# An adaLN block with RG-LRU, forgetting attention and SwiGLU: the upper feed-forward products with tokens standing and 512 weight columns moving

## The chip, the cores and the metric

The kernel runs on one core of a Trainium2 chip. The metric is the device time in microseconds (us); the median of three runs of the kernel before is 2051.7. Engines are called PE (TensorE), DVE (VectorE), ACT (ScalarE), POOL (GpSimd) and SP (SyncE, which here issues DMA transfers); PEld is TensorE's weight load, which overlaps its matmuls.

## The reference

One transformer-like block on 512 tokens of width 2048, in float32. Around it lie six modulation vectors from the condition `c`; the sixth, gt2, gates the last residual add:

```python
mod = c_act @ w_ada[l] + b_ada[l]
sh1, sc1, gt1, sh2, sc2, gt2 = jnp.split(mod, 6, axis=-1)
h = modulate(rms_norm(x, g_mix[l]), sh1, sc1)
proj = h @ w_in[l]
...
x = x + gt1[:, None, :] * (mix @ w_out[l])
h2 = modulate(rms_norm(x, g_ffn[l]), sh2, sc2)
gate, up = jnp.split(h2 @ w_up[l], 2, axis=-1)
x = x + gt2[:, None, :] * ((jax.nn.silu(gate) * up) @ w_down[l])
```

Between `proj` and `mix` stand a gated linear recurrence and an attention with forget gates. `w_up` is 2048 x 11264 (gate and up halves of 5632 = 44 x 128 features), `w_down` 5632 x 2048.

## The kernel before

Every large product is made of float32 data split in two: a high part (an ACT copy that rounds, L234) and a low part (a DVE subtraction, L235), and three matmuls: high by high, high by low, low by high. Raw weights come by DMA into buffers of 128x2048 (two in the pool `raw`, two in `raw2`); halves of 1024 are split into rings of three pages each for the high and the low parts (`wsplit`). So a split waits until TensorE is done with the third split before it.

The program runs through these stages: the input projection, the attention heads, the recurrence, the output projection wo0 to wo3 (from 540.6 us to 724.4), two groups of feed-forward features by ordinary products (up0, up1), the other 40 features of 128 each by fast products ("upper", 816 to 1622 us), and the down projection in four phases (1622 to 2044 us). During the early stages DVE also works off a queue of modulation blocks: `ada_block` loads 128x2048 of `w_ada` in two halves and multiplies and sums them against the broadcast `c_b` (L159, L169); tables such as `WO_ADA` say at which steps a block is taken from the queue.

The upper products use the seven products of a fast 2x2 scheme: gate and up features by token halves of 256, input dimension in halves. For each feature block f the weights (four blocks of 128x512 per chunk, two chunks) are summed on DVE (L1108, L1109, L1112), split, and then used as the standing operand: 128x128 of weights stand, 256 tokens move, 168 matmuls a feature (L1131). The token combinations, called T[p] and in the rows ta to tg, were split earlier. Four PSUM banks hold the seven products of a feature, and its results are formed by DVE (L1146 to L1150, L1152) and ACT (L1151), with features on the partitions, as the down projection wants them. `keep_act` then folds pairs of results for the down phases and sends them to DRAM (`td`).

In the same loop 64 pieces of gt2 (128x512, L189) are taken one after each chunk, loaded through ACT's DMA queue, and the sums of down weights that two products want (`s2d`, `s4d`) are made by accumulating DMA.

The down phases also use seven products: 4 and 5, then 1 and 7, then 6, then 2 and 3, each over q = 0 to 10. In a step q of the first two phases the first product's weights lie in `raw`, the second's in `raw2`; the second's are the sum of both, made in place on DVE (L1187). In phase 0 the order on all engines is product 4 of q, product 5 of q, product 4 of q + 1. Each product of a step is 24 matmuls of 512 columns with tokens standing (`dn_mm`, through L239).

The order of each engine's instructions comes from the order of the code, moved by priorities (`AHEAD` = 2000 puts loads and splits ahead, `EVAC` = 2500 the copies that free PSUM) and by `issue_after`, which ties an instruction behind another.

## Time and profile before

| what | value |
|---|---|
| runs of the kernel before | 2051.39, 2051.70, 2052.81 us (median 2051.7) |
| the profiled execution | 2049.87 us |
| its span in the trace | 2048.2 us |
| PE / DVE / ACT busy | 2030.6 / 1707.4 / 944.7 us |
| granted TensorE clock | 0.998 |
| upper products, 816 to 1622 us | PE 806.00 busy, DVE 711.65, ACT 341.32 |
| down phase 0, 1622 to 1742 us | PE 118.67 busy, DVE 91.96 |
| down phase 1, 1742 to 1862 us | PE 120.00 busy, DVE 90.38 |

The busy time of an engine counts its instructions' own time, waits left out. The chain of work that ended last is followed back from the last instruction, at each step to what released it; the share of an engine in it says how much of the span it set. In a timeline a row gives the start and length of an instruction, its line in the code, its output and inputs (without buffer numbers), and in brackets how long its engine had been idle and what ended that. For a DMA, landing is counted from its issue.

### The profile page before, as it was taken

To read this page: it belongs to the slowest core of one execution; us is meant where nothing else is said; L and a number is where in the kernel's file an instruction comes from. 1 tells how busy PE (TensorE), PEld (TensorE's weight loads), DVE (VectorE), ACT (ScalarE), POOL (GpSimd) and SP (SyncE) were. 2 spreads that over 40 slices of the span, in tenths; PEclk is the share of its full clock that TensorE was granted. 3 is DMA by queue.
4 is the path that set the end of the run, shared out by engine and by line. 5 is a ranking of instruction groups with operands and counts; after the bars stand their busy time and mean duration, and the time that the engine had idled before them with its cause. 6 is when DMAs were issued, how large, how long until landed. Compare 5 with 4: busy or idle time off the path is not lost.

```text
span 2048.2 us, 32491 instructions
## 1 busy us (share of the span) xinstructions
PE 2030.6 (99%) x12529; PEld 1850.5 (90%) x12529; DVE 1707.4 (83%) x2560; ACT 944.7 (46%) x1321; POOL 98.1 (5%) x126
## 2 busy tenths in 40 slices
PE   9999999999999999999999999999999999999999
PEld 7889998888888888999999999999999978888887
DVE  8999769887687669888898888989888877777796
ACT  4433447765522266444444444444444355545443
POOL 0000000111000000001000000000000000000000
PEclk9999999999999999999999999999999999999999
DMA  9989766767588852448988888988888587777894
GB/s 351 356 299 328 247 224 225 228 210 260 181 294 302 286 175 101 134 134 235 264 230 239 238 232 246 251 244 232 245 235 227 165 281 236 238 252 240 280 326 167
DMA packets 175822, 493.36 MB, mean 241 GB/s; under 512 B 20625, under 2 KB 45105, under 8 KB 171570
## 3 DMA queue, kind: packets, MB, share of 16 engines
q1 hardware_dynamic: 156162, 437.68, 63.1%
q0 software_dynamic: 10144, 36.70, 9.6%
q10 hardware_dynamic: 9360, 16.89, 2.4%
q8 instruction: 98, 1.61, 0.3%
q14 instruction: 58, 0.48, 0.1%
...
## 4 chain that ended last, share of the span: by engine, by line
PE 90%; DVE 4%; issue 2%; DMA 2%; SPq 0%; ACT 0%; POOL 0%; DVEq 0%; ACTq 0%; POOLq 0%
PE w1p L239 4%; PE dn6p L239 3%; PE dn3p L239 3%; PE dn2p L239 3%; PE dn7p L239 3%; PE dn1p L239 3%; PE dn5p L239 3%; PE dn4p L239 2%; PE yr1p L239 2%; PE up0p L239 2%; PE yr0p L239 2%; PE wo2p L239 2%; PE wo3p L239 2%; PE wo1p L239 2%; PE up1p L239 2%
## 5 line engine op out<-in xcount | busy, mean ns | idle before, releaser
L159 DVE SCALAR_TENSOR_TENSOR ada<-ada,c_b 128x1024 f32<-128x1024 f32 x96 | 116.1, 1220 | 26.6 <-DMA ada<-in_adaT 26.5
L234 ACT ACTIVATE uq_0sh<-uq_0r 128x1024 fp32r<-128x1024 f32 x40 | 42.4, 1060 | 116.9 <-DVE uq_0r L1109 113.8
L235 DVE TENSOR_TENSOR uq_0tl<-uq_0r,uq_0th 128x1024 fp32r<-128x1024 f32 x40 | 49.0, 1224 | 37.3 <-ACT uq_0th L234 37.3
L234 ACT ACTIVATE uq_0ah<-uq_0r 128x1024 fp32r<-128x1024 f32 x40 | 42.4, 1060 | 69.2 <-PE uf37p L1131 2.1
L234 ACT ACTIVATE uq_1ah<-uq_1r 128x1024 fp32r<-128x1024 f32 x40 | 42.5, 1062 | 60.6 <-issue 26.3
L235 DVE TENSOR_TENSOR uq_0al<-uq_0r,uq_0ah 128x1024 fp32r<-128x1024 f32 x40 | 49.0, 1224 | 25.5 <-ACT uq_0ah L234 24.2
L1048 POOL DMA_DIRECT2D s2d<-in_wdn x44 | 36.4, 826 | 668.1 <-DMA s2d<-in_wdn 641.1
L235 DVE TENSOR_TENSOR uq_0sl<-uq_0r,uq_0sh 128x1024 fp32r<-128x1024 f32 x40 | 49.0, 1226 | 18.8 <-ACT uq_0sh L234 18.3
L234 ACT ACTIVATE uq_0th<-uq_0r 128x1024 fp32r<-128x1024 f32 x40 | 42.4, 1060 | 45.1 <-DVE uq_0sl L235 2.5
L1151 ACT ACTIVATE ug<-ug 128x512 f32<-128x512 f32 x40 | 25.3, 632 | 81.2 <-DVE ug L1148 81.2
L234 ACT ACTIVATE uq_1th<-uq_1r 128x1024 fp32r<-128x1024 f32 x40 | 42.4, 1061 | 33.8 <-PE uf43p L1131 1.1
L234 ACT ACTIVATE uq_1sh<-uq_1r 128x1024 fp32r<-128x1024 f32 x40 | 42.5, 1062 | 25.3 <-DVE uq_1r L1109 23.8
L235 DVE TENSOR_TENSOR uq_1tl<-uq_1r,uq_1th 128x1024 fp32r<-128x1024 f32 x40 | 48.9, 1222 | 4.9 <-ACT uq_1th L234 3.8
L239 PE MATMUL w1p<-hpl,w1h 128*128 128x512 f32 x128 | 49.8, 389 | 0.0
L239 PE MATMUL w1p<-hph,w1l 128*128 128x512 f32 x128 | 49.8, 389 | 0.0
L235 DVE TENSOR_TENSOR uq_1sl<-uq_1r,uq_1sh 128x1024 fp32r<-128x1024 f32 x40 | 49.0, 1224 | 0.1
L1108 DVE TENSOR_TENSOR uq_0r<-uq_0r 128x1024 f32<-128x1024 f32 x40 | 48.7, 1218 | 0.0
L235 DVE TENSOR_TENSOR uq_1al<-uq_1r,uq_1ah 128x1024 fp32r<-128x1024 f32 x40 | 48.7, 1217 | 0.0
L1108 DVE TENSOR_TENSOR uq_1r<-uq_1r 128x1024 f32<-128x1024 f32 x40 | 48.7, 1217 | 0.0
L189 DVE SCALAR_TENSOR_TENSOR gt<-gt,c_b 128x512 f32<-128x512 f32 x64 | 43.8, 684 | 0.0
L169 DVE SCALAR_TENSOR_TENSOR ada<-ada,c_b 128x1024 f32<-128x1024 f32 x32 | 39.0, 1218 | 5.0 <-DMA ada<-in_adaT 4.9
L239 PE MATMUL w1p<-hph,w1h 128*128 128x512 f32 x128 | 42.4, 391 | 0.0
...
## 6 DMA issues: line engine op xcount, KB each, us to landing
ada<-in_adaT SPq DMA_DIRECT2D x128, 512.0 KB, 5.1
...
gt<-in_adaT ACTq DMA_DIRECT2D x64, 256.0 KB, 5.9
...
```

Of the source, the lines that this page charges most:

```text
L159: nc.vector.scalar_tensor_tensor(out=t, in0=t, scalar=1.0, in1=cs, op0=ALU.mult, op1=ALU.mult, accum_out=ac)
L169: nc.vector.scalar_tensor_tensor(out=t, in0=t, scalar=1.0, in1=c_b[:, cs], op0=ALU.mult, op1=ALU.mult, accum_out=ada_acc[j][:, hf, i:i + 1])
L189: nc.vector.scalar_tensor_tensor(out=t, in0=t, scalar=1.0, in1=c_b[:, r * S:(r + 1) * S], op0=ALU.mult, op1=ALU.mult, accum_out=gt2_acc[:, ...
L234: tail_hi.append(nc.scalar.activation(R(hi[:, :n]), raw_ap, AF.Copy).ins)
L235: tail_lo.append(nc.vector.tensor_sub(R(lo[:, :n]), raw_ap, hi[:, :n]).ins)
L239: nc.tensor.matmul(ps, lhsT=R(l), rhs=R(r), start=start, stop=stop)
L1048: nc.gpsimd.dma_start(out=out[:, cs], in_=src[:, cs], accum_op=ALU.add)
L1108: nc.vector.tensor_add(blocks[:, 0:3:2], blocks[:, 0:2], blocks[:, 2:3].broadcast_to([P, 2, 512]))
L1151: nc.scalar.activation(g, g, AF.Silu)
```

## The change

**Upper products.** The loop over 40 features becomes one over 10 blocks of four features (512 columns). In a block the seven products come one after another, in the order 4, 5, 1, 7, 6, 2, 3. The token combinations are now the standing operand (128x128 of the two halves t), and 512 weight columns move: 48 matmuls a product through the helper `mm` (L245 of the new code), two PSUM banks each. The weights come as four units A, C, B, D of 128x4096 (in two tiles); they are relaid in DRAM for this. Between the products they are summed in place on DVE, 2048 wide (L1130): A += C for product 5, C += B for 7, A += B for 6, D += A for 3. They are split in quarters of 1024. Results now have tokens on the partitions: ACT copies products 4, 5, 1 and 7 out (L1197), DVE folds (L1204, L1206 to L1209, L1214), and the result of Silu (L1217) by the other half (L1218) is turned back by four TensorE transposes a feature into the one bank `rg` (`back`, L1159) and copied by ACT (L1162). The transposes of a block stand in products 5 and 1 of the next; those of the last block in down phase 0.

**Buffers.** `raw2` has four buffers instead of two. `c_b` and some sums move to a pool that ends before the upper products; `c_b` is kept in DRAM and loaded again, in one of `raw2`'s buffers, in down phase 0.

**gt2.** Its first six k-tiles join the queue of modulation blocks (12 operations of 128x1024; `WO_ADA` and the hooks of the stage before wo0 take more blocks at other steps). The other ten make 40 pieces of 128x512 (L194), two a step, from step 2 of down phase 0 to the end of phase 1.

**Down phases.** Phase 0 is skewed: product 4 of q + 1 comes ahead of product 5 of q. The loading of a step (`dn_open`) is parted from its splits (`dn_prod`). The accumulating DMA of `s2d` and `s4d` is spread at other steps of the upper loop (`SUMS_AT`, `SUMS_PER`).

```diff
-WO_ADA = ((11, 14), (0, 4, 8, 12), (0, 3, 6, 9, 12), (0, 3, 6, 9))
+WO_ADA = ((9, 12, 15), (0, 3, 6, 9, 12), (0, 3, 6, 9, 12, 15), (0, 2, 4, 6, 8))
-GT2_AT, SUMS_AT = 16, 14
+GT2_ADA = 6
+SUMS_AT, SUMS_PER = 24, 10
...
+    for i in range(GT2_ADA):
+        pending.append(((GT2, i), lambda i=i: ada_block(GT2, i)))
...
-    bp = ctx.enter_context(tc.tile_pool(name="bp", bufs=2))
+    bp = ctx.enter_context(tc.tile_pool(name="bp", bufs=4))
...
+    ORDER = (4, 5, 1, 7, 6, 2, 3)
...
+    def sum_unit(dst, src):
+        for d_, s_ in zip(dst, src):
+            nc.vector.tensor_add(d_, d_, s_)
...
+            elif p == 5:
+                sum_unit(un[U_A], un[U_C])
...
+        for q in range(4):
+            with tc.high_priority(offset=AHEAD):
+                hi, lo = wsplit(src[q // 2][:, (q % 2) * 1024:(q % 2 + 1) * 1024], 1024, f"up{b}_{p}_{q}")
...
+    def back(g, b, f, last=False):
+        pt = misc(f"up_t{b}_{f}") if last and f else rgp(f"up_t{b}_{f}")
+        for t in range(NT):
+            nc.tensor.transpose(out=pt[:, t * P:(t + 1) * P], in_=g[t][:, f * P:(f + 1) * P], identity=ident)
+        o = page(f"uo{b}_{f}", "d")
+        with tc.high_priority(offset=EVAC):
+            nc.scalar.activation(o, pt, AF.Copy)
+        keep_act(o, 2 * STD + 4 * b + f)
...
-                for k in range(4):
-                    th, tl = T[p][c * 4 + k]
-                    ks = slice(k * P, (k + 1) * P)
-                    for n, (w, x) in enumerate(((hi, th), (hi, tl), (lo, th))):
-                        first, last = c + k + n == 0, c == 1 and k == 3 and n == 2
-                        nc.tensor.matmul(m[p], lhsT=R(w[:, ks]), rhs=R(x), start=first and p in opens, stop=last,
-                                         skip_group_check=True)
+            for j, hi, lo in prod_weights(p, b, un):
+                th, tl = T[p][j]
+                for t in range(2):
+                    c_ = slice(t * P, (t + 1) * P)
+                    mm(ps[t], th[:, c_], hi, j == 0, False)
+                    mm(ps[t], th[:, c_], lo, False, False)
+                    mm(ps[t], tl[:, c_], hi, False, j == 7)
+                for fn in hk.get((i, j), ()):
+                    fn()
...
+        hk = {(1, 1 + 2 * f): [lambda g=s1 + u2, b=b, f=f: back(g, b, f)] for f in range(4)}
...
+        steps = [(q, n) for q in range(NQ) for n in range(len(prods))]
+        if ph == 0:
+            steps.sort(key=lambda x: (x[0] + x[1], x[1]))
...
+                for m in range(2 * (NQ * ph + q - GT2_AT), 2 * (NQ * ph + q - GT2_AT) + 2):
+                    if 0 <= m < 4 * (KT - GT2_ADA):
+                        gt2_piece(m)
```

How the instructions stand now is shown at three places. First TensorE in the upper products. Before, in feature 12 (`uq_0a` and `uq_0c` are weight parts, the trailing h and l mean high and low; `tb` and `tc` are token combinations):

```order
L1131 MATMUL uf12p_9575<-tb2h,uq_0ah 128x256
L1131 MATMUL uf12p_9575<-tb2l,uq_0ah 128x256
L1131 MATMUL uf12p_9575<-tb2h,uq_0al 128x256
L1131 MATMUL uf12p_9575<-tb2h,uq_0ah 128x256
L1131 MATMUL uf12p_9575<-tb2l,uq_0ah 128x256
L1131 MATMUL uf12p_9575<-tb2h,uq_0al 128x256
L1131 MATMUL uf12p_9573<-tc0h,uq_0ch 128x256
```

Now, from the end of product 4 to the start of product 5 of a block (`up_5_0h` are weights, `td0h` tokens, `us_1` results of the block before):

```order
L245 MATMUL up_4p_9465<-up_4_3l,te7h 128x512
L245 MATMUL up_4p_9465<-up_4_3h,te7l 128x512
L245 MATMUL up_5p_9546<-up_5_0h,td0h 128x512
L245 MATMUL up_5p_9547<-up_5_0h,td0h 128x512
L1159 MATMUL up_t_0_9566<-ident,us_10_9146 128x128
L245 MATMUL up_5p_9546<-up_5_0l,td0h 128x512
L245 MATMUL up_5p_9546<-up_5_0h,td0l 128x512
L245 MATMUL up_5p_9547<-up_5_0l,td0h 128x512
```

The operand behind the arrow that moves has 512 columns instead of 256, a product runs to its end before the next begins, and product 5 opens with two matmuls of the high part and a transpose, ahead of the first that wants the low part.

Second DVE in the upper products. Before, between features 12 and 14 (`uq` weights, `ug` and `uu` results, `gt2_3` a piece of gt2):

```order
L235 TENSOR_TENSOR uq13_1sl_9944<-uq13_1r_9930,uq13_1sh_9943 128x1024
L1152 TENSOR_TENSOR ug12_9805<-ug12_9805,uu12_9806 128x512
L235 TENSOR_TENSOR uq13_1tl_9949<-uq13_1r_9930,uq13_1th_9948 128x1024
L189 SCALAR_TENSOR_TENSOR gt2_3_9689,gt2_acc_130<-gt2_3_9689,c_b_81 128x512
L235 TENSOR_TENSOR uq14_0al_10070<-uq14_0r_10066,uq14_0ah_10069 128x1024
L1106 TENSOR_TENSOR uq14_1cl_10187<-uq14_1r_10179,uq14_1ch_10186 128x512
L1108 TENSOR_TENSOR uq14_0r_10066<-uq14_0r_10066 128x2x512
L1109 TENSOR_TENSOR uq14_0r_10066<-uq14_0r_10066 128x512
```

Now, ahead of product 5 of block 3 (`uw3_00` and `uw3_01` are the halves of unit A, `uw3_1` those of C, `uw3_2` of B; `us2`, `uu2` results of block 2; `up3_5_0l` is the first low part of product 5):

```order
L1218 TENSOR_TENSOR us2_11_9148<-us2_11_9148,us2_41_8948 128x512
L241 TENSOR_TENSOR up3_4_1l_9495<-uw3_00_9466,up3_4_1h_9494 128x1024
L1214 TENSOR_TENSOR uu2_0_9296<-up2_3p0_9388,uu2_0_9296 128x512
L1214 TENSOR_TENSOR uu2_1_9297<-up2_3p1_9389,uu2_1_9297 128x512
L241 TENSOR_TENSOR up3_4_2l_9511<-uw3_01_9469,up3_4_2h_9510 128x1024
L1130 TENSOR_TENSOR uw3_00_9466<-uw3_00_9466,uw3_10_9472 128x2048
L241 TENSOR_TENSOR up3_4_3l_9527<-uw3_01_9469,up3_4_3h_9526 128x1024
L1130 TENSOR_TENSOR uw3_10_9472<-uw3_10_9472,uw3_20_9674 128x2048
L1130 TENSOR_TENSOR uw3_01_9469<-uw3_01_9469,uw3_11_9475 128x2048
L241 TENSOR_TENSOR up3_5_0l_9551<-uw3_00_9466,up3_5_0h_9550 128x1024
```

Small sums and splits of one feature are replaced by sums of 2048, three of which stand ahead of the split that product 5 begins with, among the folding of the block before.

Third DVE in down phase 0 (`dq4_6r` is product 4's raw weights of step 6, `w0l` and `w1l` the low parts of its halves, `tl` of the tokens). Before:

```order
L235 TENSOR_TENSOR dq5_5w0l_17794<-dq5_5r_17774,dq5_5w0h_17793 128x1024
L235 TENSOR_TENSOR dq5_5w1l_17798<-dq5_5r_17774,dq5_5w1h_17797 128x1024
L1185 TENSOR_TENSOR dq4_6tl_17852<-dq4_6tl_17852,dq4_6th_17853 128x512
L235 TENSOR_TENSOR dq4_6w0l_17864<-dq4_6r_17849,dq4_6w0h_17863 128x1024
L235 TENSOR_TENSOR dq4_6w1l_17868<-dq4_6r_17849,dq4_6w1h_17867 128x1024
L1185 TENSOR_TENSOR dq5_6tl_17858<-dq5_6tl_17858,dq5_6th_17859 128x512
L1187 TENSOR_TENSOR dq5_6r_17855<-dq5_6r_17855,dq4_6r_17849 128x2048
L235 TENSOR_TENSOR dq5_6w0l_17875<-dq5_6r_17855,dq5_6w0h_17874 128x1024
L235 TENSOR_TENSOR dq5_6w1l_17879<-dq5_6r_17855,dq5_6w1h_17878 128x1024
```

Now:

```order
L1259 TENSOR_TENSOR dq5_4tl_14018<-dq5_4tl_14018,dq5_4th_14019 128x512
L1261 TENSOR_TENSOR dq5_4r_14015<-dq5_4r_14015,dq4_4r_14009 128x2048
L241 TENSOR_TENSOR dq5_4w0l_14152<-dq5_4r_14015,dq5_4w0h_14151 128x1024
L241 TENSOR_TENSOR dq5_4w1l_14156<-dq5_4r_14015,dq5_4w1h_14155 128x1024
L1259 TENSOR_TENSOR dq4_6tl_14186<-dq4_6tl_14186,dq4_6th_14187 128x512
L241 TENSOR_TENSOR dq4_6w0l_14198<-dq4_6r_14183,dq4_6w0h_14197 128x1024
L241 TENSOR_TENSOR dq4_6w1l_14202<-dq4_6r_14183,dq4_6w1h_14201 128x1024
L194 SCALAR_TENSOR_TENSOR gt2_8_14058,gt2_acc_133<-gt2_8_14058,c_b2_13788 128x512
L194 SCALAR_TENSOR_TENSOR gt2_9_14142,gt2_acc_133<-gt2_9_14142,c_b2_13788 128x512
L1259 TENSOR_TENSOR dq5_5tl_14105<-dq5_5tl_14105,dq5_5th_14106 128x512
L1261 TENSOR_TENSOR dq5_5r_14102<-dq5_5r_14102,dq4_5r_14096 128x2048
```

The sum of step 5 (`dq5_5r` with `dq4_5r`) stood ahead of step 6's splits of product 4 and stands behind them now, with two pieces of gt2 between.

More of the change, by code (lines that the diff above doesn't have):

```diff
@@ L911, in x1_fin @@
         nc.vector.scalar_tensor_tensor(out=t, in0=t, scalar=mods[GT1][:, kt:kt + 1], in1=xt, op0=ALU.mult, op1=ALU.add)
-    bu_acc = [cp.tile([P, S], F32, name=f"bu_acc{gi}", tag="ssq", bufs=2) for gi in range(STD)]
+    bu_acc = [rsp.tile([P, S], F32, name=f"bu_acc{gi}", tag="ssq", bufs=2) for gi in range(STD)]
     bu_src = {}
@@ new lines, in block_kernel, with load_unit @@
+    bp = ctx.enter_context(tc.tile_pool(name="bp", bufs=4))
+    U_A, U_C, U_B, U_D = range(4)
+    IN_RAW = (2, 4, 9, 11)
+    ORDER = (4, 5, 1, 7, 6, 2, 3)
+    NBLK = (FT - 2 * STD) // 4
+    loads = []
+    def load_unit(b, u):
+        tiles = []
+        mine = len(loads) % 12 in IN_RAW
+        loads.append((b, u))
+        for hf in range(2):
+            nm = f"uw{b}_{u}{hf}"
+            if mine:
+                t = wp.tile([P, 2048], F32, tag="raw", name=nm, bufs=RAW)
+            else:
+                t = bp.tile([P, 2048], F32, tag="raw2", name=nm)
+            for i in range(2):
+                cs = slice(i * 1024, (i + 1) * 1024)
+                ld = nc.sync.dma_start(out=t[:, cs], in_=wups[b, u, :, hf * 2048 + i * 1024:hf * 2048 + (i + 1) * 1024])
+            up_loads.append(ld.ins)
+            tiles.append(t)
+        return tiles
@@ L1155, in block_kernel @@
+    up_tail = [lambda g=s1 + u2, b=b, f=f: back(g, b, f, True) for f in range(4)]
     PHASES = (((4, 3, 1), (5, 2, 0)), ((1, 0, 0), (7, 2, 1)), ((6, -2, 0),), ((2, 1, 0), (3, -4, 1)))
```

261 lines of the change are left out of this document (151 added, 110 removed).

## The prediction

> **What bounds the kernel now.** I read first the busy shares and the chain of work that ended last.
>
> ```profile
> span 2048.2 us, 32491 instructions
> ...
> PE 2030.6 (99%) x12529; PEld 1850.5 (90%) x12529; DVE 1707.4 (83%) x2560; ACT 944.7 (46%) x1321; POOL 98.1 (5%) x126
> ...
> PE 90%; DVE 4%; issue 2%; DMA 2%; SPq 0%; ACT 0%; POOL 0%; DVEq 0%; ACTq 0%; POOLq 0%
> ```
>
> TensorE sets the end: it works 99% of the span and is 90% of the chain. So time falls only where TensorE's work falls, and rises wherever it is made to wait. The next view is the table by stage: duration, then busy time of PE, PEld, DVE, ACT and POOL, granted clock, DMA share. The first two rows are the upper products, the last two the first two down phases.
>
> ```profile
> 816.00:1219.00 403.00, 403.00 (x3361) 403.00 (x3359) 354.12 (x492) 170.85 (x202) 24.84 (x30) 1.00 0.74 211
> 1219.00:1622.00 403.00, 403.00 (x3361) 403.00 (x3360) 357.53 (x522) 170.47 (x200) 29.53 (x36) 1.00 0.82 232
> 1622.00:1742.00 120.00, 118.67 (x523) 97.34 (x522) 91.96 (x86) 58.22 (x71) 0.00 (x0) 1.00 0.75 252
> 1742.00:1862.00 120.00, 120.00 (x532) 99.34 (x531) 90.38 (x78) 61.03 (x75) 0.00 (x0) 1.00 0.72 238
> ```
>
> In the upper products TensorE has no gap and VectorE is busy 88% (711.65 of 806 us): little slack beside the bound. The clock is full, so no part of the change can win clock.
>
> **The change, part by part. Matmuls.** The chain in order of time gives the paces (start, length, what, count); x1p are transposes of the kind that the change adds.
>
> ```profile
> 815.97 20.15 PE uf4p L1131 x168
> 836.12 20.16 PE uf5p L1131 x168
> ...
> 1646.36 5.44 PE dn4p L239 x24
> ...
> 626.59 1.75 PE x1p L900 x16
> ```
>
> A matmul that moves 256 columns costs 20.16/168 = 0.1200 us, one that moves 512 costs 5.44/24 = 0.2267 us. Two halves cost 0.2400, so 0.0133 us goes with each matmul whatever its width. The 40 features took 40 x 20.16 = 806.4 us; the new loop has 10 x 7 x 48 = 3,360 matmuls of 512 columns, 761.6 us: **-44.8**.
>
> [...]
>
> **Transposes.** Ten blocks of 16 are new. Sixteen in a row took 1.75 us, 0.109 each: 160 x 0.109 = **+17.5**. One alone is longer:
>
> ```profile
> L900 PE MATMUL x1p<-ident,x 128*128 128x128 f32 x64 | 7.6, 272 | 0.0
> L903 ACT ACTIVATE x1w<-x1p 128x512 f32<-128x512 f32 x16 | 9.4, 603 | 1.7 <-PE x1p L900 1.7
> ```
>
> The 272 ns are a length, not a spacing; if they did not overlap, the price would be 160 x 0.272 = 43.5. I take the spacing, since the new ones too stand in a stream that does not wait. [...]
>
> The four groups of a block share one bank. From one group to the next only about four matmuls (0.91 us) cover its copy (0.60 us, and ScalarE may be in the middle of a split of 1.06 us). Between 0 and 3 x 1.1 us per block; I take 0.3, since the copy usually fits, for nine blocks: **+2.7**.
>
> **The border between two blocks.** Here VectorE has to sum and split weights and to fold results at once. Its rows in order of time (start, length):
>
> ```profile
> 1000.93 0.69 DVE L1147 TENSOR_TENSOR uw<-ug,uf12p 128x512 f32<-128x512 f32 x1
> 1001.54 1.22 DVE L235 TENSOR_TENSOR uq_1al<-uq_1r,uq_1ah 128x1024 fp32r<-128x1024 f32 x1
> 1002.67 0.68 DVE L1106 TENSOR_TENSOR uq_0cl<-uq_0r,uq_0ch 128x512 fp32r<-128x512 f32 x1
> 1003.28 1.22 DVE L1108 TENSOR_TENSOR uq_1r<-uq_1r 128x1024 f32<-128x1024 f32 x1
> 1004.41 0.42 DVE L1148 TENSOR_TENSOR ug<-uf12p,uw 128x256 f32<-128x256 f32 x1
> ...
> 1755.32 2.28 DVE L1187 TENSOR_TENSOR dq_1r<-dq_1r 128x2048 f32<-128x2048 f32 x1
> ```
>
> Neighbours overlap by about 0.08 us: 512 elements come every 0.61 us, 1024 every 1.14, so I put 2048 at 2.20. From product 6's end VectorE does 10.8 us of work, then waits for product 2 (48 x 0.2267 = 10.88 us). From there to product 5's first low part stand thirteen operations of 512 (7.9), six of 1024 (6.8), three of 2048 (6.6), and the split itself (1.22): 10.88 + 22.5 = 33.4 us after product 6's end. TensorE begins product 5 at 3 x 10.88 = 32.64, and can do two high matmuls and a transpose (0.56) first: it wants the low part at 33.2. With something for the last matmul to drain I take 0.4 us at each of nine borders: **+3.6**. Below, with 1 us saved somewhere, it is zero; above, at full lengths (0.68, 1.22, 2.28), it is 35.7 - 33.2 = 2.5 us each.
>
> **Down phase 0.** The new skewed order puts the sum of product 5 of step n (which reads product 4's raw weights) behind the splits of product 4 of step n+1, while these raw weights have two buffers. So the load for step n+2 can start only when that sum ends, and the next sum can come only after that load was split: a loop. Its pieces, from VectorE in order of time, SyncE's issues, and the view by tile:
>
> ```profile
> 1678.56 0.68 DVE L1185 TENSOR_TENSOR dq_5tl<-dq_5tl,dq_5th 128x512 fp32r<-128x512 f32 x1
> 1679.16 2.28 DVE L1187 TENSOR_TENSOR dq_5r<-dq_5r 128x2048 f32<-128x2048 f32 x1
> 1682.70 1.23 DVE L235 TENSOR_TENSOR dq_5w0l<-dq_5r,dq_5w0h 128x1024 fp32r<-128x1024 f32 x1 [1.26 <-ACT dq_5w0h L234]
> 1683.84 1.22 DVE L235 TENSOR_TENSOR dq_5w1l<-dq_5r,dq_5w1h 128x1024 fp32r<-128x1024 f32 x1
> 1684.98 0.69 DVE L1185 TENSOR_TENSOR dq_6tl<-dq_6tl,dq_6th 128x512 fp32r<-128x512 f32 x1
> ```
>
> ```profile
> 1681.50 4.39 SPq L1162 DMA_DIRECT2D dq_7r<-in_wdn  x4
> ```
>
> ```profile
> L1162 SPq DMA_DIRECT2D dq_7r<-in_wdn x4: 328/378/424, 1681.5 to 1685.5; - x4
> DMA to landing us min/median/max: 3.5/4.2/4.8
> ```
>
> For step 4, where more was under way, the same view has:
>
> ```profile
> L1162 SPq DMA_DIRECT2D dq_4r<-in_wdn x4: 328/382/433, 1648.9 to 1652.8; - x4
> DMA to landing us min/median/max: 5.5/6.1/6.3
> ```
>
> Issue 0.06 after the sum (1681.50 against 1681.44), landing L, high part 1.26, two low parts 2 x 1.14, two pieces of gt2 1.22, a token split 0.60, the sum 2.28: L + 7.7 us per step, where TensorE needs 48 x 0.2267 = 10.88. With L from 3.5 to 5.5 that is 0.3 to 2.3 us a step; before, a whole step more lay between the load and its use. I take L = 4.0, since the half that is wanted first lands early: 0.82 x 9 steps = **+7.4** (2.9 to 20.9). Of the 1.22 us of gt2 this holds all; without them L would have to pass 4.4.
>
> **gt2 elsewhere.** Its 64 pieces leave the upper loop:
>
> ```profile
> L189 DVE SCALAR_TENSOR_TENSOR gt<-gt,c_b 128x512 f32<-128x512 f32 x64 | 43.8, 684 | 0.0
> ...
> gt<-in_adaT ACTq DMA_DIRECT2D x64, 256.0 KB, 5.9
> ```
>
> In down phase 1 two pieces a step (1.22 us) come ahead of product 7's sum; TensorE has three to four high matmuls to bridge that. Between 0 and 0.4 us at 11 steps: **+2**. The first pair is issued just ahead of its use; its 5.9 us landing is partly in view, 0 to 3 us: **+1.5**. Six k-tiles go to the earlier stages as 12 operations of 1024 (13.7 us by 1.14). These stages have room:
>
> ```profile
> 490.00:541.00 51.00, 51.00 (x232) 41.10 (x231) 35.09 (x62) 24.05 (x43) 2.88 (x5) 1.00 0.60 208
> 541.00:588.00 47.00, 46.91 (x222) 38.70 (x221) 40.19 (x64) 20.41 (x29) 2.01 (x2) 1.00 0.68 231
> ```
>
> VectorE is idle 16 of 51 us and 7 of 47; a piece in the way of an output ratio may cost 0 to 3: **+1**. **The seam to the down phases**: TensorE idles 1.33 us there (120.00 - 118.67); the skew brings product 4 twice before product 5's sum is wanted, which covers it: **-1.2**.
>
> **Sum**: -44.8 + 17.5 + 2.7 + 3.6 + 7.4 + 2 + 1.5 + 1 - 1.2 = -10.3. The profiled execution took 2049.87 us (span 2048.2, and 1.7 around it), so 2039.6; it lies 1.8 below the median of the runs, 2051.7, so I forecast **2041.4 us**.
>
> **The rivals.** *All waits stay hidden.* Border, loop and gt2 cost nothing: 2051.7 - 44.8 + 17.5 - 1.2 = 2023.2. For it: VectorE has less to do per feature than before (gt2 is gone). Against: the loop is longer than the step even at the shortest landing.
>
> *Slower: the border is VectorE's at its full lengths.* If operations that read what the one before wrote do not overlap, or ScalarE's high parts come between, it is 2.5 us a border: 2041.4 + 9 x 2.1 = 2060.3. It decides from 2.0 us a border (without that term the sum is -13.9; +4.1 is what a measurement of this kernel can tell, 0.2%). For it: 88% busy already. Against: row 1000.93 to 1001.54 shows the overlap right behind a bank read.
>
> *No change: the loop with slow landings.* Two loads more a step in a stage whose DMA share is 0.75: L = 5.5, as in step 4, gives 2041.4 + 13.5 = 2054.9, L = 5 gives 2050.4. Against: in step 7, deep in the stage, the longest landing was 4.8.
>
> *The matmul keeps its pace per column* (0.2400 for 512): nothing is saved, 2041.4 + 44.8 = 2086.2. The 512-column row excludes it, unless the new order of operands matters. [...]
>
> *Transposes at their length*: 2041.4 + 26 = 2067.4, if each interrupts the stream. Against: 16 in 1.75 us.
>
> **How the numbers follow.** Forecast 0.52 (2032 to 2047, all faster), all hidden 0.16, border 0.13, slow landings 0.14, the matmul's price 0.02, the transposes' 0.03. Of slow landings 0.03 still end faster, 0.08 within 0.2%, 0.03 slower; of the border 0.04 within. Faster 0.71, same 0.12, slower 0.17. The range: below, the forecast without the border's and the transposes' waits and the loop at 2.9 gives 2030.6, and half of the all-hidden case is taken in, 2026; above, the border to 2.4 us, 2059.
>
> **What would show it.** Right: a product of the upper loop takes 10.88 us plus its transposes, PE's gaps stand at each product 5 (0.2 to 0.6 us) and at product 4 or 5 of down phase 0 (0.3 to 1.2 us a step), and SyncE waits there for the sum on VectorE. Wrong: a 512-column matmul in that loop at another pace than 0.2267, PE gaps of over 2 us a border, or gaps in the stages ahead of the upper loop, which the sum has at 1 us.

## The result and the profile after

The changed kernel takes 2083.46 us (four runs, 2078.00 to 2085.13) against 2051.59 for the kernel before on the same chip: a ratio of 1.0149, interval 1.013 to 1.0168. It is slower by 31.9 us, where 2041.4 with a range of 2026 to 2059 was forecast. The profiled execution took 2083.25 us. Its page opens with the span and the busy times:

```profile
span 2081.5 us, 25602 instructions
...
PE 2034.3 (98%) x9329; PEld 1695.5 (81%) x9329; DVE 1678.2 (81%) x2276; ACT 982.2 (47%) x1361; POOL 100.1 (5%) x127
```

TensorE has 3,200 instructions fewer and is yet busy no shorter (2034.3 us against 2030.6), though matmuls and transposes were to take 27.3 us off it; the sum over the span does not tell where the time went. So I cut the span where each stage's first matmul starts. Phase 2 ends here at product 3's first matmul and so holds product 2's first step of 5.4 us too:

| stage | before, us | after, us | difference | forecast |
|---|---|---|---|---|
| attention heads | 345.3 | 350.4 | +5.1 | } |
| ahead of wo0 | 50.4 | 54.2 | +3.8 | } +1 |
| wo0 | 47.9 | 49.0 | +1.1 | } |
| upper products | 806.4 | 805.3 | -1.1 | -22.8 |
| down phase 0 | 121.9 | 133.0 | +11.1 | +9.5 |
| down phase 1 | 119.7 | 124.2 | +4.5 | +2 |
| down phase 2 | 65.5 | 74.1 | +8.6 | 0 |
| the rest of the span | 491.1 | 491.3 | +0.2 | 0 |

The transposes of the tenth block stand in down phase 0, so of the +17.5 for 160 of them 15.7 (144) belong to the upper products and 1.8 (16) to phase 0: -44.8 + 15.7 + 2.7 + 3.6 and 7.4 + 1.5 - 1.2 + 1.8. The view by windows gives the stages that differ (length, then busy time of PE, PEld, DVE, ACT and POOL with their instructions, granted clock, DMA share, GB/s): ahead of wo0, the upper products, down phases 0, 1 and 2.

```profile
495.00:549.30 54.30, 52.42 (x230) 41.53 (x229) 38.96 (x71) 24.39 (x45) 3.72 (x5) 0.97 0.67 234
825.70:1631.00 805.30, 790.99 (x3505) 646.47 (x3504) 641.43 (x621) 378.04 (x439) 54.55 (x66) 0.99 0.72 200
1631.00:1764.00 133.00, 127.12 (x545) 99.29 (x544) 107.20 (x127) 62.93 (x79) 0.00 (x0) 1.00 0.79 263
1764.00:1888.30 124.30, 123.18 (x530) 98.25 (x529) 102.44 (x125) 58.04 (x72) 0.00 (x0) 1.00 0.82 275
1888.30:1962.40 74.10, 69.52 (x290) 55.93 (x289) 44.59 (x50) 32.01 (x37) 0.00 (x0) 0.93 0.76 262
```

Two things stand out. In the upper products PE is idle 14.3 us, where it had no gap before, and yet VectorE is busy for 641 of 805 us, less than the 712 of before. And the clock is below 1 in three of these stages. Inside the upper products two stretches of one block's length show both:

```profile
906.00:987.00 81.00, 81.00 (x366) 66.57 (x365) 67.09 (x65) 38.94 (x45) 5.20 (x6) 1.00 0.70 199
987.00:1068.00 81.00, 76.06 (x329) 61.60 (x328) 58.70 (x59) 34.62 (x41) 5.76 (x7) 0.96 0.72 202
```

The first has no gap and the full clock. In the second 37 matmuls fewer got done in the same time. The view of waits for the upper products names who made PE wait, and for ScalarE what it waited for most (us in total, times, longest):

```profile
PE up_7p L245 <- ACT up_2h L240: 10.3, 6, 4.5
PE up_7p L245 <- DVE up_2l L241: 4.0, 6, 0.8
```

```profile
ACT us L1197 <- DMA td<-tu: 52.2, 9, 9.9
```

All of PE's waits stand in product 7, at the split of its third quarter, in six blocks; the border between blocks, where the forecast looked for VectorE, shows none. The waits for VectorE's low part `up_2l` follow from the others: on the page VectorE stands idle 76.4 us ahead of these splits, 76.3 of them for ScalarE's `up_2h`. ScalarE's rows in order of time say how the two lines hang together (idle time before an instruction in brackets, and what ended it):

```profile
1011.45 1.08 ACT L1197 ACTIVATE us<-up_5p 128x512 f32<-128x512 f32 x2
1012.40 1.07 ACT L240 ACTIVATE up_1h<-uw 128x1024 fp32r<-128x1024 f32 x1
1023.34 0.60 ACT L1197 ACTIVATE us<-up_1p 128x512 f32<-128x512 f32 x1 [9.87 <-DMA td<-tu]
1023.84 1.05 ACT L240 ACTIVATE up_2h<-uw 128x1024 fp32r<-128x1024 f32 x1
```

The copy of product 1's result (L1197) goes to a page, as the code calls a buffer of the pool `c`. The pages are used in turn: the one it gets last held `tu`, a folded pair that `keep_act` (L1043) had made, and it is free only when its store to DRAM has landed. ScalarE stands 9.87 us at that copy, and behind it in its order stands `up_2h`, the high part that product 7 needs. Two answers by tile give the stores' landings (from issue, min, median, max), the first around this block (990 to 1030 us), where accumulating transfers for `s2d` and `s4d` were issued up to 1011.3, the second in a late one (1490 to 1530 us), whose stores were issued from 1501.8 to 1512.9, in a pause between the accumulating transfers of 1498.4 and 1525.6:

```profile
DMA to landing us min/median/max: 5.8/11.1/13.2
```

```profile
DMA to landing us min/median/max: 5.0/6.9/7.4
```

TensorE's rows in the same place:

```profile
1020.07 0.39 PE L245 MATMUL up_7p<-up_1h,te3l 128*128 128x512 f32 x1
1024.93 0.79 PE L245 MATMUL up_7p<-up_2h,te4h 128*128 128x512 f32 x1 [4.47 <-ACT up_2h L240]
...
1027.21 0.63 PE L245 MATMUL up_7p<-up_2h,te4h 128*128 128x512 f32 x1
1027.64 0.63 PE L245 MATMUL up_7p<-up_2l,te4h 128*128 128x512 f32 x1
```

From start to start 4.86 us pass where 0.2267 would, and then the matmuls come every 0.43 us instead of 0.2267: the clock is at half for 6.8 us. In blocks 2 to 7 (counted from 0) these starts are 4.86, 2.19, 2.77, 0.93, 0.98 and 0.92 us apart, and the next ones 1.26 each; less the pace that is 17.5 us of stall. The first three were followed by half clock, for 6.8, 3.4 and 6.8 us. Half of that would be 8.5, but part of it lies in the second of these gaps and is counted there. The lengths of the blocks, from one product 4 to the next, give the whole without that: the six take 24.9 us more than six blocks without a gap (78.25 each), so the clock's share is some 7.4.

### The profile page after: what moved, and what is told of

Read it like the earlier page. It is cut to its first block, busy times and chain, and to the rows that moved or that the text cites. A ratio compares the mean times of both kernels' runs of the same rounds, so it can differ in the third digit from the quotient of the medians.

```text
span 2081.5 us, 25602 instructions
## 1 busy us (share of the span) xinstructions
PE 2034.3 (98%) x9329; PEld 1695.5 (81%) x9329; DVE 1678.2 (81%) x2276; ACT 982.2 (47%) x1361; POOL 100.1 (5%) x127
## 3 DMA queue, kind: packets, MB, share of 16 engines
q0 software_dynamic: 10144, 36.70, 10.4%
## 5 line engine op out<-in xcount | busy, mean ns | idle before, releaser
L1130 DVE TENSOR_TENSOR uw<-uw,uw 128x2048 f32<-128x2048 f32 x80 | 181.9, 2283 | 0.0
L241 DVE TENSOR_TENSOR up_2l<-uw,up_2h 128x1024 fp32r<-128x1024 f32 x70 | 85.4, 1220 | 76.4 <-ACT up_2h L240 76.3
L240 ACT ACTIVATE up_1h<-uw 128x1024 fp32r<-128x1024 f32 x70 | 74.5, 1064 | 103.6 <-PE up_7p L245 23.3
L241 DVE TENSOR_TENSOR up_1l<-uw,up_1h 128x1024 fp32r<-128x1024 f32 x70 | 85.5, 1222 | 43.4 <-ACT up_1h L240 43.0
L240 ACT ACTIVATE up_0h<-uw 128x1024 fp32r<-128x1024 f32 x70 | 74.2, 1060 | 87.1 <-PE up_5p L245 17.8
L240 ACT ACTIVATE up_3h<-uw 128x1024 fp32r<-128x1024 f32 x70 | 74.3, 1062 | 72.8 <-PE up_2p L245 16.6
L240 ACT ACTIVATE up_2h<-uw 128x1024 fp32r<-128x1024 f32 x70 | 74.1, 1059 | 70.4 <-PE up_2p L245 17.1
L241 DVE TENSOR_TENSOR up_3l<-uw,up_3h 128x1024 fp32r<-128x1024 f32 x70 | 85.4, 1220 | 17.2 <-ACT up_3h L240 16.3
L241 DVE TENSOR_TENSOR up_0l<-uw,up_0h 128x1024 fp32r<-128x1024 f32 x70 | 85.3, 1219 | 17.0 <-ACT up_0h L240 16.9
L245 PE MATMUL w1p<-hpl,w1h 128*128 128x512 f32 x128 | 49.8, 389 | 0.0
L245 PE MATMUL w1p<-hph,w1l 128*128 128x512 f32 x128 | 49.8, 389 | 0.0
L245 PE MATMUL w1p<-hph,w1h 128*128 128x512 f32 x128 | 42.6, 392 | 0.0
L171 DVE SCALAR_TENSOR_TENSOR adf<-adf,c_b 128x1024 f32<-128x1024 f32 x32 | 39.0, 1219 | 0.4 <-DMA adf<-in_adaT 0.3
L1197 ACT ACTIVATE us<-up_1p 128x512 f32<-128x512 f32 x20 | 11.8, 594 | 53.1 <-DMA td<-tu 52.2
L1162 ACT ACTIVATE uo<-up_t 128x512 f32<-128x512 f32 x40 | 23.6, 596 | 19.9 <-PE up_t L1159 19.9
L245 PEld LDWEIGHTS w1p<-hph,w1h 128*128 128x128 f32 x128 | 24.0, 188 | 5.4 <-issue 0.5
L245 PEld LDWEIGHTS w1p<-hph,w1l 128*128 128x128 f32 x128 | 24.0, 188 | 5.0
```

The source lines that it names most:

```text
L171: nc.vector.scalar_tensor_tensor(out=t, in0=t, scalar=1.0, in1=c_b[:, cs], op0=ALU.mult, op1=ALU.mult, accum_out=ada_acc[j][:, hf, i:i + 1])
L240: tail_hi.append(nc.scalar.activation(R(hi[:, :n]), raw_ap, AF.Copy).ins)
L241: tail_lo.append(nc.vector.tensor_sub(R(lo[:, :n]), raw_ap, hi[:, :n]).ins)
L245: nc.tensor.matmul(ps, lhsT=R(l), rhs=R(r), start=start, stop=stop)
L1130: nc.vector.tensor_add(d_, d_, s_)
L1162: nc.scalar.activation(o, pt, AF.Copy)
```

## The experiments

My theory: the upper products lose some 25 us by ScalarE's in-order wait for a page; down phase 0 loses by the loop that the prediction described; phase 2 and the early stages by two edits that it priced near zero. The rival for the upper products is VectorE, whose low parts PE waited for as well (the 4.0 us above); the other rivals are named with their runs. Stage lengths are cut as above.

**The copy moved behind product 7's splits.** `e1` makes the copies of product 1 after product 7's high parts; a page that is late then holds up nobody whom TensorE needs. `e2` keeps the order and leaves out the accumulating transfers of `s2d` and `s4d` (so the down phases read sums that are not there); the stores should land sooner.

```diff
-            if p in (4, 5, 1, 7):
+            if p == 1:
+                ps1 = ps
+            elif p in (4, 5, 7):
+                if p == 7:
+                    keep_[1] = []
+                    for t in range(2):
+                        w = page(f"us{b}_1{t}", "c")
+                        with tc.issue_after(tail_hi[-1]), tc.high_priority(offset=EVAC):
+                            nc.scalar.activation(w, ps1[t], AF.Copy)
+                        keep_[1].append(w)
```

> The changed kernel, only that ScalarE's two copies of product 1 (its result out of PSUM) stand behind the splits of product 7 instead of between them. Theory A (the copy waits for a page that the store of a fold still holds, and the splits of product 7 are queued behind it on ScalarE): the gaps inside product 7 go, with them the halved clock of the upper products; that stage falls from 805.3 us to 779 to 782 us, the run from 2083 to 2055 to 2061 us. [...] Rival C (product 7 waits for its own weights' sum or load): no change, 805 us.

```diff
-        elif n < 3:
-            dram_sum(s2d[q], wdn[n + 1, q])
-        else:
-            dram_sum(s4d[q], s2d[q])
```

> The changed kernel without the accumulating transfers that sum the down weights of products 6 and 3 in DRAM (their first copies stay; the sums are left out). Theory A with a landing time: the stores land in 6 to 7 us as in blocks 0 and 8, the wait of ScalarE for them stays but falls to about 4 us, and no gap is left in product 7: upper products 779 to 782 us. If pages and the queue of issues alone set it, whatever else is under way: the waits of 8 to 10 us stay and the stage stays above 800 us.

`e1` took 2055.61 us (ten runs), 1.0016 of the kernel before (1.0005 to 1.0026); `e2`, one run, 2050.53. The upper products of `e1` and of `e2` in the view by windows:

```profile
824.80:1605.40 780.60, 780.59 (x3506) 642.11 (x3505) 641.73 (x621) 379.99 (x439) 54.48 (x66) 1.00 0.74 206
```

```profile
820.70:1601.20 780.50, 780.50 (x3506) 642.08 (x3504) 641.94 (x621) 378.83 (x439) 0.00 (x0) 1.00 0.50 162
```

No gap and the full clock in both, with the same VectorE work as in the changed kernel. Around the same block the stores of `e2` land sooner, by the view of the tile:

```profile
DMA to landing us min/median/max: 5.6/6.4/7.2
```

One change of order on ScalarE, and independently faster stores, each give back 25 us. That settles the cause against VectorE: the wait for the page, made long by stores that land late beside the accumulating transfers. (What it is in these transfers that delays a store, the bytes or the accumulating, no run parts.) In `e2` the same copy still waits, 3.8 us at most, and no PE gap follows: it is the length that decides.

**The loop of down phase 0.** `e3` gives product 4's raw weights the pool with four buffers and product 5's the one with two, on the changed kernel. Theory: the loop opens, and what is left is VectorE's own order.

```diff
-                raws.append(dn_load("raw2" if n or (len(prods) == 1 and q % 2) else "raw", blk, q, nm + "r"))
+                raws.append(dn_load("raw2" if (n == 0 if ph == 0 else n or (len(prods) == 1 and q % 2)) else "raw", blk, q, nm + "r"))
```

> The changed kernel, only that in down phase 0 the raw weights of product 4 lie in the pool with four buffers (one of them taken by the condition) and those of product 5 in the pool with two. Theory L (the loop of load, splits, gt2 and sum through the two buffers of product 4): the phase falls from 133 us to 122 to 124 us, the run by 9 to 11 us to 2072 to 2075 us. Rival G (VectorE has simply too much to do there with the two pieces of gt2): the phase stays at 130 us or more, the run within 3 us of 2083.

It took 2072.99 us, 1.0096 (1.0073 to 1.0119), with down phase 0 at 130.8 instead of 133.0. The 122 to 124 that I expected for the phase failed, and that the run fell into the expected 2072 to 2075 is luck: its profiled execution is 7.5 us shorter than the changed kernel's, and the phase has 2.2 of them. In the changed kernel the loop had been there as forecast. SyncE's issues of product 4's raw weights for three steps, each as soon as a sum on VectorE has ended, follow each other after 12.29 and 11.74 us, where the forecast had 4.0 + 7.7 = 11.7; the first half of these weights landed after 3.8 to 4.1 us from step 5 on, as assumed (the tile of step 7 has both products' landings). The third view is the longest of SyncE's waits ahead of these weights, the fourth the two longest of PE's nine waits in the phase:

```profile
1667.02 0.87 SPq L1229 DMA_DIRECT2D dq_4r<-in_wdn  x2
...
1679.31 0.81 SPq L1229 DMA_DIRECT2D dq_5r<-in_wdn  x2
...
1691.05 0.82 SPq L1229 DMA_DIRECT2D dq_6r<-in_wdn  x2
```

```profile
DMA to landing us min/median/max: 4.1/4.9/5.9
```

```profile
SPq L1229 <- DVE dq_9r L1261: 7.0, 1, 7.0
```

```profile
PE dn5p L245 <- DVE dq_1w0l L241: 1.7, 1, 1.7
PE dn5p L245 <- ACT dq_10w0h L240: 1.0, 1, 1.0
```

With the pools exchanged, the view of PE's waits keeps these two lines alone, the first step and the last, and both are longer:

```profile
PE dn5p L245 <- DVE dq_1w0l L241: 2.0, 1, 2.0
PE dn5p L245 <- ACT dq_10w0h L240: 1.8, 1, 1.8
```

At each step between there had been two gaps, one of 0.41 to 1.00 us from start to start and one of 0.45 to 0.69; one of 0.38 to 0.48 is left. But a stretch of half clock followed the gap at step 1 (3.4 us, so 1.7 lost; the granted clock of the phase is 0.99, in the changed kernel 1.00), which takes back a part: without it the phase would be 129.1. So opening the loop is worth 2.2 to 3.9 us, and more than as much lies elsewhere.

**gt2's pieces.** `e7`, on `e1`, leaves out the 40 pieces in the down phases (so gt2 lacks their part). With them moves what waited for the last of them: the write of gt2 to DRAM, below, is issued at 676 us instead of behind phase 1. The rival is that the loop costs its price by itself, with the pools and the skew as they are.

```diff
-                        gt2_piece(m)
```

> The kernel with the late copy, only that the 40 pieces of gt2 in the down phases are left out, loads and all. By the loop as predicted (landing + 7.7 us, without the pieces landing + 6.5): phase 0 falls from 133 us to 122 to 125, as the landing would have to pass 4.4 us for a wait; phase 1 falls from 124.0 to 119.7 to 120.2, as 11 waits of 0.25 us and the first are the pieces' alone. If transfers and not VectorE hold phase 0: 129 us or more. The gap in step 0 of phase 2 (2.2 us) goes if the lateness of VectorE puts the folding ahead of the low part, and stays if the order alone does.

One run, 2035.74 us. Down phases 0, 1 and 2 by windows:

```profile
1607.10:1729.70 122.60, 122.08 (x545) 100.51 (x544) 96.06 (x91) 63.02 (x78) 0.00 (x0) 1.00 0.75 256
1729.70:1849.40 119.70, 119.70 (x529) 99.07 (x528) 90.45 (x78) 59.29 (x72) 0.00 (x0) 1.00 0.71 244
1849.40:1914.90 65.50, 65.50 (x290) 53.98 (x289) 43.47 (x49) 32.23 (x37) 0.00 (x0) 1.00 0.76 265
```

Phases 1 and 2 are back at the lengths of before, and phase 0 is within 0.7 of it, less than its 16 transposes take, although the pools and the skew are unchanged: the loop costs nothing without the 1.22 us of pieces in it, as the prediction said of it. The pieces and the write cost 10.4 us in phase 0, 4.3 in phase 1 and 8.3 in phase 2 (against `e1`: 133.0, 124.0 and 73.8). The write was not free at its new place: wo3, where it now falls, took 51.6 us instead of 45.3, with a TensorE gap of 3.97 us.

**gt2's turn.** When its last piece is summed, gt2 lies with features on the partitions and is written to DRAM turned (L1293), by 2,048 pieces of 4 bytes. In the kernel before, it was issued at 1615.9 us, ahead of the down phases; now at 1881.74, ahead of the seam to phase 2. SyncE's rows there, and the ScalarE instruction that waits:

```profile
1881.74 0.39 SPq L1293 DMA_DIRECT2D gt2d<-mod  x1
1882.22 4.23 SPq L1245 DMA_DIRECT2D dq_1tl<-td  x1
```

```profile
1897.70 0.63 ACT L1257 ACTIVATE dq_1th<-dq_1tl 128x512 fp32r<-128x512 f32 x1 [10.37 <-DMA dq_1tl<-td]
```

The tokens of step 1, issued right behind the write, are split 15.5 us after their issue began. The view of DMA for 1881 to 1900 us shows what the transfer engines moved in that time (40 slices of 0.475 us, and the packets):

```profile
GB/s 362 362 267 285 198 285 259 379 397 287 52 6 1 0 0 0 0 0 0 56 73 35 47 22 30 13 26 17 39 34 86 35 86 194 233 172 285 306 423 427
DMA packets 2958, 2.74 MB, mean 144 GB/s; under 512 B 2162, under 2 KB 2162, under 8 KB 2958
```

For some ten us little is moved, while 2,162 of the 2,958 packets of this view are small. The kernel before has the same hole behind its own write at 1615.9 (1615 to 1635 us, slices of 0.5), at a seam where TensorE lost 1.3 us in all:

```profile
GB/s 0 229 344 287 238 369 401 233 11 3 0 0 0 0 0 16 45 12 25 8 16 12 8 12 12 12 12 20 66 361 270 205 233 266 369 401 418 418 385 459
```

TensorE pays twice in the changed kernel:

```profile
1893.88 0.73 PE L245 MATMUL dn6p<-dq_0w1l,dq_0th 128*128 128x512 f32 x2 [1.82 <-DVE dq_0w1l L241]
...
1899.32 1.22 PE L245 MATMUL dn6p<-dq_1w0h,dq_1th 128*128 128x512 f32 x2 [2.72 <-ACT dq_1w0h L240]
```

The first gap is VectorE's: eight foldings of product 7 (L1367, L1368) stand ahead of that low part; in `e7`, without the pieces, they stand behind it and the gap is gone. The second is the write's. The clock is at half for 10.2 us from 1895.16 on; the second gap (3.35 from start to start) lies in it, so that some 3.5 are lost by the clock itself. Gaps of 2.21 and 3.35 less the pace, and 3.5, are the 8.6 us of the phase. Two runs ask whether SyncE's queue or the transfer itself is the matter: `e4` sends the write in four parts through GpSimd's queue and reads it back later, on the changed kernel; `e6`, on `e1`, turns gt2 by one TensorE transpose, so that 16 rows of 512 bytes are written.

```diff
-        nc.sync.dma_start(out=gd.rearrange("k p -> p k"), in_=mods[GT2])
+        for a in range(4):
+            nc.gpsimd.dma_start(out=gd[4 * a:4 * a + 4].rearrange("k p -> p k"), in_=mods[GT2][:, 4 * a:4 * a + 4])
...
```

> The changed kernel, only that the turned write of gt2 (2048 pieces of 4 bytes) goes out through GpSimd's queue, in four parts, and its reading back stands four steps later. Theory S (the write holds SyncE's queue, so that the tokens of step 1 of phase 2 land 15 us after their issue): the gap of 3.4 us before step 1 of phase 2 goes, and the half clock of 10 us with it; from the start of phase 2 to that of phase 3 it takes 67 to 69 us instead of 74.1, the run is at 2076 to 2079 us. Rival V (VectorE's folding of product 7 ahead of the low part of step 0 is the cause): the gap before step 1 stays, 73 us or more.

```diff
-        nc.sync.dma_start(out=gd.rearrange("k p -> p k"), in_=mods[GT2])
+        pt, o = acc("gt2t"), page("gt2o", "d")
+        nc.tensor.transpose(out=pt[:KT, :P], in_=mods[GT2], identity=ident)
+        nc.scalar.activation(o[:KT, :P], pt[:KT, :P], AF.Copy)
+        nc.sync.dma_start(out=gd, in_=o[:KT, :P])
```

> The kernel with the late copy, only that gt2 is turned by one transpose on TensorE and written in 16 rows of 512 bytes instead of 2048 pieces of 4 bytes. Theory S2 (the pieces keep the transfer engines busy for some 10 us whichever queue issues them, and what comes behind lands late): tokens of step 1 of phase 2 land within 6 us, the gap ahead of step 1 and the half clock go, the phase falls from 73.8 us to 67 to 68.5 (a gap of 2 us on VectorE's folding in step 0 stays), the run by 5 to 7 us. Rival (the landing is late for the loads around it): 72 us or more.

`e4` took 2085.34 us, 1.0155 (1.0133 to 1.0177), and phase 2 grew to 80.0: my expectation failed. Another queue did not free the tokens' load, though only the first quarter of the write was issued ahead of it (1879.87 us; the load 1880.03, split at 1895.1), and there were new waits further on:

```profile
ACT dq_1th L1257 <- DMA dq_1tl<-td: 9.5, 1, 9.5
ACT dq_7th L1257 <- DMA dq_7tl<-td: 7.0, 1, 7.0
```

So SyncE's queue is not the cause; what is left is the transfer. `e6` took 2047.83 us, 0.9984 (0.9975 to 0.9994), with phase 2 at 67.4 and no ScalarE wait for a transfer in it. Its write came at 1863.95 us, later than the tokens' load, so what it does to others is read from the weights issued 0.9 us behind it (the tile `dq_4r`):

```profile
DMA to landing us min/median/max: 4.0/4.4/4.8
```

Weights issued 5 us behind the turned write of the changed kernel took 12.9 to 13.9 us. The hole behind the small pieces stands in the changed kernel and in the kernel before (the two rows of GB/s above); over phase 2 as a whole the transfer engines moved 281 GB/s in `e6`, 262 in the changed kernel. `e6` is the first version faster than the kernel before, by 0.16%. The 1.9 us that remain in phase 2 are the first gap (2.0 from start to start), VectorE's order.

**The early stages.** VectorE's, ScalarE's and TensorE's rows at the border of the heads and the stage ahead of wo0:

```profile
490.89 1.23 DVE L161 SCALAR_TENSOR_TENSOR ada<-ada,c_b 128x1024 f32<-128x1024 f32 x1 [2.46 <-DMA ada<-in_adaT]
...
495.94 1.22 DVE L161 SCALAR_TENSOR_TENSOR ada<-ada,c_b 128x1024 f32<-128x1024 f32 x1 [1.53 <-DMA ada<-in_adaT]
...
497.09 0.75 DVE L535 COPY qk<-h7p 128x256 f32<-128x256 f32 x2
```

```profile
497.54 0.28 ACT L538 ACTIVATE v<-h7p 128x128 f32<-128x128 f32 x1 [3.90 <-DVE qk L535]
```

```profile
497.87 0.50 PE L245 MATMUL yr1p<-hh,yr_0h 128*128 128x512 f32 x1 [1.88 <-ACT v L538]
```

A modulation block whose load has not landed stands on VectorE ahead of a copy out of the last head's PSUM bank (L535); ScalarE's copy of the rest of that bank (L538) follows it, and TensorE waits for the bank. Half clock for 3.4 us follows, from 499.11 on: 2.1 for the gap and 1.7 for the clock are the 3.8 of this stage. `e5`, on `e1`, moves the three blocks of that stage to later steps; `e10`, on `e1`, leaves out gt2's six k-tiles altogether, with the steps of the kernel before (so gt2 lacks their part).

```diff
-    for n in (3, 8, 11):
+    for n in (6, 10, 13):
```

> The kernel with the late copy (first experiment), only that the three modulation blocks in the stage ahead of wo0 are taken at steps 6, 10 and 13 instead of 3, 8 and 11. Theory M (a block whose load has not landed stands on VectorE ahead of the copies that free the last head's banks): the gap of 2 us at that stage's start goes, with the half clock beside it; the stage falls from 54 to 55 us to 50.4 to 51.5, the run by 2.5 to 4.5 us. Rival W (too much work for VectorE there, wherever it stands): the stage stays within 1 us.

```diff
-WO_ADA = ((9, 12, 15), (0, 3, 6, 9, 12), (0, 3, 6, 9, 12, 15), (0, 2, 4, 6, 8))
+WO_ADA = ((11, 14), (0, 4, 8, 12), (0, 3, 6, 9, 12), (0, 3, 6, 9))
...
-    for i in range(GT2_ADA):
-        pending.append(((GT2, i), lambda i=i: ada_block(GT2, i)))
...
-    for n in (3, 8, 11):
-        add(hk, n, ada1)
+    add(hk, 8, ada1)
```

> The kernel with the late copy, only that the six k-tiles of gt2 are left out of the early stages (gt2 is then short of them) and the blocks are taken as in the kernel before. Theory M (these blocks alone lengthen the two stages from the last head to wo0): the stage ahead of wo0 is back at 50.4 to 51 us from 54.9, wo0 at 47.9 to 48.2 from 49.6. Rival N (the moved pools and buffers do it): 54 us and 49.

`e5` took 2055.05 us, 1.0014 (1.0002 to 1.0025), no other than `e1`, so that my expectation failed: the gap moved to a later place (2.43 us from start to start at 534) and the stage kept 54.1. `e10`, one run, 2049.47, has wo0 at 47.9 and this stage as before, without a gap:

```profile
492.30:542.70 50.40, 50.40 (x229) 40.53 (x229) 34.48 (x62) 23.41 (x42) 2.89 (x5) 1.00 0.57 204
```

So it is the number of blocks in that stage; at both places tried it cost the same. The heads are another matter: they have half clock without the change too, 6.8 us of it in the kernel before and 13.7 in the changed kernel (stage lengths from 345.1 to 350.4 over all kernels), so of their +5.1 nothing is shown to be the change's.

**Putting it together.** `e8` joins `e1`, `e3`, `e6` and `e5`'s steps. `e9` (with the three blocks back at steps 3, 8 and 11) spreads the pieces, one a step in phase 0, two in phase 1, one in phase 2, and so turns gt2 only at the end of phase 2 and moves foldings of phase 2 to phase 3. `e11` is `e9` with one block ahead of wo0 instead of three and two in up0. `e12` is `e8` with eight k-tiles early, one block ahead of wo0 and four in up0, and all pieces from step 1 of phase 0 to the end of phase 1.

> Late copy, the two pools of down phase 0 swapped, gt2 turned on TensorE and the blocks taken at steps 6, 10 and 13, together. If the four causes are apart from each other, the sum of their stages: upper products 781, phase 0 129, phase 2 67 to 68, the stage ahead of wo0 51: the run at 2036 to 2043 us, 0.4 to 0.8% under the kernel before. If one wait only covers another: 2048 or more.

```diff
-                for m in range(2 * (NQ * ph + q - GT2_AT), 2 * (NQ * ph + q - GT2_AT) + 2):
-                    if 0 <= m < 4 * (KT - GT2_ADA):
-                        gt2_piece(m)
...
+                for _ in range((int(q >= GT2_AT), 2, int(q < 9), 0)[ph]):
+                    gt2_piece(gt2_n[0])
+                    gt2_n[0] += 1
...
-                if (ph, q) == (2, 2):
+                if (ph, q) == (2, 10):
                     gt2_spread()
...
+            if (ph, q, n) == (3, 2, 1):
+                for a in later:
+                    finish(*a)
```

> Late copy, swapped pools and gt2 turned on TensorE as in the eighth experiment (the blocks of the early stages as in the changed kernel), and the 40 pieces of gt2 spread thinner: one a step in phase 0 from step 2, two a step in phase 1, one a step in phase 2 up to step 8; the last folding with gt2 moves into phase 3. If two pieces a step are what VectorE cannot hold in phase 0 (gaps of 0.25 us a step and 2 us at its end): phase 0 falls from 129.5 to 123 to 126 us, phase 1 stays at 124, phase 2 at 66 to 68: the run at 2040 to 2044 us. If the two buffers, wherever they lie, hold phase 0: 129 us again and 2047.

```diff
-    for n in (3, 8, 11):
-        add(hk, n, ada1)
+    add(hk, 8, ada1)
...
+            add(hk, 1, ada1)
+            add(hk, 5, ada1)
```

> The ninth experiment's kernel, only that the six blocks of gt2 come last in the queue, behind those of the scale; two are taken in the stage of the ordinary upper products, and the stage ahead of wo0 takes one block as before. By theory M that stage falls from 54 to 55 us to 50.4 to 51.5, wo0 stays at 49 to 50, up0 grows by 0 to 1: 3 to 4 us under the ninth, 2036 to 2041 us. By rival N no gain.

```diff
-GT2_ADA = 6
+GT2_ADA = 8
...
-    for n in (6, 10, 13):
-        add(hk, n, ada1)
+    add(hk, 8, ada1)
...
+            for n in (1, 4, 7, 10):
+                add(hk, n, ada1)
...
+                for _ in range((int(q >= 1), 2, 0, 0)[ph]):
```

> The four mends in the form that the runs so far favour: late copy, swapped pools, gt2 turned on TensorE, one block in the stage ahead of wo0, and gt2 with eight k-tiles in the early stages (four of them during the ordinary upper products) and 32 pieces in the down phases, one a step in phase 0 from step 1 and two a step in phase 1. By the stages of the eighth and eleventh: ahead of wo0 50.4 us, upper products 781, phase 0 123 to 124.5, phase 1 124, phase 2 67.4: the run at 2035 to 2042 us, 0.5 to 0.8% under the kernel before. If the four blocks delay the ordinary upper products' splits, up0 takes 50 us or more and the run is at 2043 to 2047.

| kernel | us | ratio (interval) | ahead of wo0 | up0 | phase 0 | phase 1 | phase 2 |
|---|---|---|---|---|---|---|---|
| before | | | 50.4 | 48.1 | 121.9 | 119.7 | 65.5 |
| e6 | 2047.83 | 0.9984 (0.9975 to 0.9994) | 54.7 | 48.6 | 131.6 | 124.0 | 67.4 |
| e8 | 2046.99 | 0.9979 (0.9969 to 0.9989) | 55.2 | 48.0 | 129.5 | 123.9 | 67.4 |
| e9 | 2050.87 | 1.0000 (0.9989 to 1.0011) | 54.8 | 50.3 | 122.8 | 123.9 | 81.4 |
| e11 | 2050.01 | 0.9989 (0.9976 to 1.0003) | 50.4 | 48.0 | 123.5 | 123.9 | 79.7 |
| e12 | 2048.99 | 0.9992 (0.9977 to 1.0006) | 50.4 | 53.9 | 126.6 | 123.9 | 67.4 |

`e8` has the lowest time, 0.2% ahead of the kernel before and not to be told from `e6` by these intervals; it stayed above the 2036 to 2043 us that I expected, since the early stages kept their loss. `e9`, `e11` and `e12` missed what I expected too (2040 to 2044, 2036 to 2041, 2035 to 2042) and are no faster than the kernel before: each won where it was aimed and lost in another place. In `e9` one piece a step brings phase 0 to 122.8, but the foldings stand in the way at the next seam, where product 3 waits 3.01 us for a sum on VectorE, with half clock behind it (matmuls 0.43 us apart up to 1937.40). (Product 2's second step comes ahead of product 3's first in `e9` and `e11`, so the column makes their loss too large; from phase 2's start to that of product 2's third step they take 94.0 and 93.5 us, `e6` 83.7.)

```profile
1934.25 0.79 PE L245 MATMUL dn3p<-dq_0w0h,dq_0th 128*128 128x512 f32 x1 [3.01 <-DVE dv L1388]
```

`e11` shows that the blocks can leave the stage ahead of wo0 at no loss in up0, but wo1 to wo3 grew from 137.6 to 139.9. In `e12` two blocks more in up0 made a gap of 3.6 us there, and there was one of 2.28 at step 1 of phase 0. No version had all its stages at their best together.

## Why the prediction was wrong, point by point

**What it costed held.** In `e1` the first block, which has no transposes, takes 76.16 us, which is 336 matmuls at 0.2267; the nine others take 78.2 to 78.4. So the pace was right. Of the 2.1 us that 16 transposes add, their spacing of 0.109 makes 1.75, so their 272 ns were a length only, and the bank that they share the other 0.34: the forecast's 0.3, +2.7, held as well. The border's +3.6 was nothing; PE's waits show none. Its upper end was also added up wrongly: at full lengths the operations make 24.2 us, so the low part comes at 35.1, 1.9 us late and not 2.5. With 1.9 in place of 2.4 the top of the range, 2059, would have been near 2055.

**The failed step is "The border between two blocks".** It asked where an engine that TensorE needs comes late, and of VectorE alone, since that was 88% busy. ScalarE entered only as the copier of transposes, with the lengths of its splits, and in a rival as late with high parts at the border. That its copies need pages, that a page is held until a store lands, and that the splits stand behind those copies in order, was not looked at; it cost 24.7 us (805.3 to 780.6), more than all the waits of the sum. No rival had it either. With this one wait gone the kernel takes 2055.6 us, inside the range, but still 0.16% slower than before where 10 us less were forecast: the other stages below make up the rest.

**The clock.** "No part of the change can win clock" was true, and left out that the change could lose some: about 7.4 us in the upper products, 3.5 in phase 2, 1.7 ahead of wo0.

**Down phase 0**, +9.5 forecast with the transposes that fall there, +11.1 measured. The loop was there, with the period and landings worked out and SyncE's waits for the sum as the prediction's sign had them, and needs the pieces of gt2 (`e7`). From step 2 to step 9 TensorE took 11.83 us a step on average, 0.95 over 10.88, where 0.82 was forecast. But that is not the loop's alone: the exchange of pools took 2.2 us off the phase, 3.9 without the half clock that it ran into, against 7.4. The rest are pieces that delay a low part at every step also without the loop, and the first pair. Its load is waited for, in `e6` as two waits on VectorE:

```profile
1625.69 0.69 DVE L194 SCALAR_TENSOR_TENSOR gt<-gt,c_b 128x512 f32<-128x512 f32 x1 [1.29 <-DMA gt<-in_adaT]
...
1626.94 0.69 DVE L194 SCALAR_TENSOR_TENSOR gt<-gt,c_b 128x512 f32<-128x512 f32 x1 [0.55 <-DMA gt<-in_adaT]
```

That is 1.8 us of VectorE's time, where +1.5 was put down; how much of it TensorE lost is not shown. The seam's -1.2 fits: in `e7` the phase is 0.7 us longer than before with 1.75 us of transposes in it.

**Down phase 1**, +2 forecast, +4.5 measured: 0.41 a step, the top of the range of 0 to 0.4 that it gave.

**Down phase 2 and the early stages.** The steps "gt2 elsewhere" priced the pieces and not what follows from their end: the turned write and its seam moved with them (+8.6). The six early k-tiles were put at +1 from VectorE's idle time; the loads that they bring, and who stands behind them on VectorE, made +4.9 (3.8 ahead of wo0 and 1.1 in it; `e10` takes both away). Idle time of an engine said nothing on the order in it. Gaps in these stages were among the forecast's own signs of being wrong.
